# A decoder layer with 16384 experts on one core: the dense half of the tokens moved from the middle to the end

## The chip, the core and the metric

The kernel runs on one core of a Trainium2 chip. A core has a tensor engine (PE; its weight loads are shown apart as PEld), a vector engine (DVE), a scalar engine (ACT), GpSimd (POOL) and a queue engine for transfers (SP). Each works through its own instructions in a fixed order and waits on semaphores for the others. Sixteen DMA engines move data between DRAM and the core; SP starts the plain transfers here, POOL the gathers by index. The metric is the device time of one execution in microseconds; lower is better.

## The reference

One layer for 1024 tokens of width 1024, all in float32: a norm, a mixer of three branches (stick-breaking attention, sparse attention in three forms, a gated linear recurrence), a merge with sigmoid gates, an output projection, a second norm, a feed-forward part with product keys, a final norm. The change concerns the feed-forward part:

```python
qh = (xc @ w_q).reshape(Ct, H, 2, PEER_QDIM // 2)
s = jnp.einsum("nhad,akd->nhak", qh, sub_keys).astype(f32)
top_s, top_i = lax.top_k(s, K)
...
best_s, pos = lax.top_k(cand, K)
eidx = jnp.take_along_axis(cand_idx, pos, axis=-1)
gate = jax.nn.softmax(best_s, axis=-1)
ug = u_tab[eidx]
vg = v_tab[eidx]
hpre = jnp.einsum("nd,nhkd->nhk", xc, ug).astype(f32)
act = (gate * jax.nn.gelu(hpre, approximate=False)).astype(x.dtype)
return jnp.einsum("nhk,nhkd->nd", act, vg)
```

Each token has 8 heads of 16 experts, that is 128 of the 16384 experts; each expert has a row of 1024 numbers in `u_tab` and one in `v_tab`.

## The kernel before

The tokens go through the mixer in four parts of 256 (`PARTS`, parts 0 to 3), one after the other. Work is emitted in steps: a step takes the next stage of several branch chains (*items*), and fills up with *pieces* that stand on their own (projections, norms, merges, scores, routes) up to an estimate of vector and tensor work (`account`, L1054). A part's *tail* (`tail_pieces`: merge of the branches, output projection, second norm; then `score_pieces` and `routes`) is placed beside the next part's items by `place_tail` (L1262). The tail of the last part has no such place; its pieces go into a list, `ending`.

A scheduler with a simulated timeline then fixes each engine's order of instructions; on the chip this order doesn't change.

The experts are computed in two ways, each for half of the tokens.

*Gathered* (`gather_tile`, L1095, a tile of 128 tokens at a time). For each of the 128 places in the list, POOL gathers a row of `u` for every token (L1104: 128 rows of 1024 numbers, called a row here), and the vector engine multiplies it with the token's activations and sums (L1106). After a Gelu and the gates, 128 rows of `v` follow (L1114), each multiplied and added to the sum (L1116). Tiles of four parts would be eight; four are gathered: 4 x 256 = 1024 rows. The rows share five buffers (tag `rows`, `RB`), one of which holds the token tile's input or its running sum. `paced` (L1075) ties a row's arithmetic to a step of the mixer, so that it isn't issued before: 420 rows from step 135 on, in proportion to a step's tensor work; the others are free after the last step.

*Dense* (L1326 on). The tokens of `DENSE = PARTS[1:3]` (L65) go through all experts, in 128 blocks of 128 experts: a first product (`gemm1`, L1327: U block times the tokens' activations in two float16 parts, 24 matmuls of 512 columns, then Gelu), a multiplication with the gates spread over all experts (L1368), a split in two float16 parts (L200 and L201, tile `ac`), a second product with the V block (`gemm2`, L1375, 24 matmuls), accumulated in seven eighths over all blocks in PSUM, the rest added by the vector engine (L1383). First products run three blocks ahead (`LEAD`). The spread gates come from `spread_pieces` (L1158): for every four tokens four one-hot operations on the vector engine (L1168 to L1171, tile `hot`), eight matmuls (L1174, L1175), a copy (L1177), and for every sixteen tokens a store of 1 MB to `d_G`.

Since the last part isn't dense, the dense blocks can start when part 2 has its routes and its spread gates. The last part's tail is put between the blocks, three pieces of `ending` to a block (`TP`, L1388), and its two tiles are gathered after that.

Of the kernel before, what the change touches and what calls it, by code (L numbers as in the profile page):

```python
# [10 lines left out]
F32 = mybir.dt.float32  # L11
# [25 lines left out]
# operands of the large products are split into two float16 parts after scaling by these powers of two  # L37
# [4 lines left out]
# scales of the gates, of their spread over the experts, and of the activations in the dense experts  # L42
# [5 lines left out]
# block numbers in the stream of projection weights  # L48
# [5 lines left out]
class Part:  # L54
    """a run of tokens that goes through the mixer together"""
# [8 lines left out]
# the parts whose tokens go through all experts; the others' experts are gathered  # L64
DENSE = PARTS[1:3]  # L65
# [4 lines left out]
def trunk(ctx: ExitStack, tc: tile.TileContext, a: dict, out: bass.AP):  # L70
# [13 lines left out]
    # what the mixer alone needs  # L84
# [44 lines left out]
    # strictly causal block in reversed key order: key 127 - x, allowed where 127 - x < p  # L129
# [3 lines left out]
    # causal block: key x allowed where p - x >= 0  # L133
# [3 lines left out]
    # for each length of segments: keys of a first half before queries of the second, the second halves' queries only  # L137
# [7 lines left out]
    # distances to the keys of the window and to the ends of the blocks, negative; far under where the key isn't seen  # L145
# [11 lines left out]
    # lower bounds: cumulative softmax over the layers less the first layer's share  # L157
# [12 lines left out]
    # the window's keys and values: this part's and the one's before  # L170
# [27 lines left out]
    def split(hi, lo, src, scale):  # L198
        """src * scale in two float16 parts"""
# [3 lines left out]
    def rms_scale(src, name, junk, tg=""):  # L203
        """1/sqrt(mean(src^2) + eps) for each of 128 rows of 1024."""
# [15 lines left out]
    def load_w(blk, name, pt, br=False):  # L220
        """a block of weights in two parts; split for the first part, kept in DRAM for the others"""
# [29 lines left out]
    def transposed(src, name, pre=False):  # L251
        """the 128-column blocks of src transposed, side by side in one bank"""
# [11 lines left out]
    def norm_rows(xt, gname, nm):  # L264
        """RMSNorm of one token tile"""
# [5 lines left out]
    def norm_cols(ht, hh, hl, tl, kk, scale, nm):  # L271
        """half of a token tile transposed into columns of hh / hl"""
# [8 lines left out]
    own_h2 = {}  # L281

    def h2_cols(pt):
        if pt.last:
            if not own_h2:
                own_h2[0] = htp.tile([128, 2, 8, pt.n], F16, tag="hT", name="h2_last")
            return own_h2[0][:, 0], own_h2[0][:, 1]
        c = (pt.t0 - TD) % TH
        return h2[:, 0, :, c:c + pt.n], h2[:, 1, :, c:c + pt.n]
# [7 lines left out]
    # Work comes in two kinds. Pieces stand on their own (projections, norms, merges); items are steps of the  # L297
    # branches' chains, each cut into four stages so that several can be under way at once.
# [37 lines left out]
    def sb_pieces(p, pt, st):  # L336
# [3 lines left out]
        def keep(t, d):  # L340
            # the tokens of earlier parts come back from DRAM
# [10 lines left out]
        # keys and values in reversed token order  # L352
# [19 lines left out]
    def sb_items(p, pt, st):  # L372
# [3 lines left out]
        def chunk(tl, hh, c0, c1, W):  # L376
# [62 lines left out]
    def nsa_kv_pieces(pt, st):  # L439
# [22 lines left out]
        # compression of keys and values: block c takes the pieces c and c + 1 of 16 tokens.  # L462
        # Two neighbouring positions lie one under the other on the partitions; columns: position pair, group, block
# [3 lines left out]
        def pieces(which):  # L467
# [13 lines left out]
            # the last piece is kept for the next part  # L481
# [48 lines left out]
    def nsa_items(g, tl, pt, st, kv):  # L530
# [9 lines left out]
        # compressed branch  # L540
        def c_logits():
# [6 lines left out]
            # a column of nothing before the first block  # L548
# [19 lines left out]
        def c_select():  # L568
            # importance of the blocks: the heads' weights of the five pieces that overlap; sure blocks at the top
# [926 lines left out]
```

## Time and profile before

| | us |
|---|---|
| median of the runs | 3744.84 |
| lowest, highest | 3733.98, 3757.71 |
| span of the profiled execution | 3722.6 |
| PE busy | 3285.9 |
| DVE busy | 3035.8 |
| ACT busy | 1572.2 |
| POOL busy | 1275.4 |

The profile shows one execution: for each instruction its line, its engine, the program's names of what it writes and reads (`out<-in`), its start and duration, and what ended the idle time before it. Times in a trace are counted from the span's start. The executions hold the span and some time around it. "Busy" of the tensor engine includes the latency of pipelined matmuls. The granted clock is the share of its full clock that the tensor engine ran at.

### The profile page before, as it was taken

The page shows a single profiled execution, that of the slowest core. Times are in us where ns is not written, and L with a number is a line of the kernel's source. Part 1 is how long each engine was busy: PE and PEld are TensorE (multiplying, and loading weights), DVE is VectorE, ACT ScalarE, POOL GpSimd, SP SyncE. Part 2 cuts the span into 40 slices and gives each one's busy share as a digit, 9 for nine tenths or more (in the row PEclk, how much of TensorE's full clock was granted, in tenths as well). Part 3 has the DMA queues.
Part 4 walks back from the last instruction along what each step waited for, and adds up shares of the span by engine and source line. Part 5 has one row for each costly group of instructions (what it writes and reads, how often), then busy time and mean ns, then how long its engine had stood idle before and what let it go on. Part 6 is the DMA issues. An engine that isn't in the chain of part 4 may idle for free. (4 is left out here: it accounts for less than half of the span.)

```text
span 3722.6 us, 57637 instructions
## 1 busy us (share of the span) xinstructions
PE 3285.9 (88%) x20660; PEld 2191.0 (59%) x20660; DVE 3035.8 (82%) x7067; ACT 1572.2 (42%) x3110; POOL 1275.4 (34%) x1167
## 2 busy tenths in 40 slices
PE   6999999999986999898878897859999999999993
PEld 5887777777875777786566453424444444444441
DVE  5665689788799888789988678988888887888886
ACT  4776456554444564554457223323232223223222
POOL 0000002343322432233222344144555554555554
PEclk9999999999995999898577999979999999999996
DMA  7964857889974878877465999579999999999987
GB/s 260 334 243 144 295 189 274 317 308 325 328 273 147 300 256 300 296 278 261 142 208 195 356 332 325 193 273 339 333 337 325 320 337 322 346 332 318 334 287 261
DMA packets 359916, 1055.48 MB, mean 284 GB/s; under 512 B 35814, under 2 KB 108330, under 8 KB 355532
## 3 DMA queue, kind: packets, MB, share of 16 engines
q0 software_dynamic: 147456, 536.94, 41.5%
q1 hardware_dynamic: 212172, 514.86, 38.7%
q8 instruction: 162, 2.65, 0.3%
q14 instruction: 126, 1.03, 0.1%
HBM read 943.66 MB, written 108.00 MB: 283 GB/s over the span
## 5 line engine op out<-in xcount | busy, mean ns | idle before, releaser
L1114 POOL DMA_INDIRECT v<-in_peer_v_dram,gidx x512 | 655.1, 1280 | 872.7 <-DVE gacc L1116 590.8
L1104 POOL DMA_INDIRECT u<-in_peer_u_dram,gidx x512 | 605.9, 1183 | 869.1 <-DVE u L1106 599.4
L242 PE MATMUL g<-h,us 128*128 128x512 f16 x3072 | 712.5, 390 | 109.0 <-DVE acc L1383 71.4
L1116 DVE SCALAR_TENSOR_TENSOR gacc<-v,act,gacc 128x1024 f32<-128x1024 f32 x512 | 654.6, 1278 | 112.2 <-DMA v<-in_peer_v_dram,gidx 104.8
L1106 DVE SCALAR_TENSOR_TENSOR u<-u,gh 128x1024 f32<-128x1024 f32 x512 | 618.1, 1219 | 124.6 <-DMA u<-in_peer_u_dram,gidx 123.2
L242 PEld LDWEIGHTS <-us 128*128 128x128 f16 x3072 | 306.1, 100 | 497.8 <-issue 115.4
L1375 PE MATMUL acc<-vs,ac 128*128 128x512 f16 x2304 | 536.3, 384 | 33.1 <-ACT ac L200 28.4
L1375 PEld LDWEIGHTS <-ac 128*128 128x128 f16 x3072 | 302.9, 99 | 414.2 <-ACT ac L200 30.9
L242 PE MATMUL pj_mg<-hT,w_mg 128*128 128x256 f16 x2304 | 279.1, 277 | 16.3 <-ACT mg L859 9.5
L242 PEld LDWEIGHTS <-w_mg 128*128 128x128 f16 x2304 | 229.5, 101 | 48.8 <-issue 20.7
L200 ACT ACTIVATE vs<-vraw 128x1024 f16<-128x1024 f32 x128 | 133.8, 1048 | 270.3 <-DMA vraw<-in_peer_v_dram 270.1
L200 ACT ACTIVATE ac<-ge 128x512 f16<-128x512 f32 x128 | 79.9, 626 | 365.8 <-DVE ge L1368 250.0
L1335 ACT ACTIVATE ge<-g 128x512 f32<-128x512 f32 x128 | 75.6, 590 | 362.7 <-PE g L242 362.6
L1375 PE MATMUL g<-vs,ac 128*128 128x512 f16 x768 | 179.5, 385 | 9.6 <-DVE ts L958 7.3
L201 DVE SCALAR_TENSOR_TENSOR vs<-vraw,vs 128x1024 f16<-128x1024 f32 x128 | 155.2, 1217 | 23.2 <-ACT vs L200 23.2
L1174 PE MATMUL gb<-hot 128*128 128x128 f16 x512 | 126.3, 295 | 44.6 <-ACT stage L1177 28.9
L1177 ACT ACTIVATE stage<-gb 128x512 f32<-128x512 f32 x128 | 131.9, 1070 | 79.0 <-DMA d_G<-stage 45.2
L200 ACT ACTIVATE us<-uraw 128x1024 f16<-128x1024 f32 x128 | 134.0, 1049 | 68.2 <-DMA uraw<-in_peer_uT_dram 52.6
L242 PE MATMUL pb<-o,w_b 128*128 128x256 f16 x1152 | 141.6, 279 | 19.4 <-DMA w_b<-dw 9.3
L201 DVE SCALAR_TENSOR_TENSOR us<-uraw,us 128x1024 f16<-128x1024 f32 x128 | 155.7, 1218 | 2.9 <-ACT us L200 2.7
L242 PE MATMUL pj_r_hg<-hT,w_r_hg 128*128 128x256 f16 x1152 | 138.2, 277 | 1.5 <-ACT iv_hg L715 0.7
L242 PEld LDWEIGHTS <-w_b 128*128 128x128 f16 x1152 | 113.8, 101 | 42.6 <-issue 14.5
(1133 smaller groups left out, 5944.0 us busy)
## 6 DMA issues: line engine op xcount, KB each, us to landing
uraw<-in_peer_uT_dram SPq DMA_DIRECT2D x128, 512.0 KB, 6.7
vraw<-in_peer_v_dram SPq DMA_DIRECT2D x128, 512.0 KB, 6.2
w_mg<-dw SPq DMA_DIRECT2D x72, 512.0 KB, 6.3
d_G<-stage SPq DMA_DIRECT2D x32, 1024.0 KB, 5.1
gt<-d_G SPq DMA_DIRECT2D x32, 1024.0 KB, 13.2
w_r_hg<-dw SPq DMA_DIRECT2D x36, 512.0 KB, 5.7
w_b<-dw SPq DMA_DIRECT2D x72, 256.0 KB, 5.9
wr_mg<-in_wblk_dram SPq DMA_DIRECT2D x24, 512.0 KB, 5.1
```

The costliest lines, as they stand in the source:

```text
L200: S.activation(hi, src, AF.Copy, scale=scale)
L201: V.scalar_tensor_tensor(lo, in0=src, scalar=scale, in1=hi, op0=ALU.mult, op1=ALU.subtract)
L242: P.matmul(ps, l[:, k, :], r[:, k, :], start=(i == 0), stop=(i == n - 1))
L1104: G.indirect_dma_start(out=ur, out_offset=None, in_=a["peer_u"], in_offset=bass.IndirectOffsetOnAxis(ap=idx[:, c:c + 1], axis=0))
L1106: V.scalar_tensor_tensor(ur, in0=ur, scalar=1.0, in1=h2, op0=ALU.mult, op1=ALU.mult, accum_out=hpre[:, c:c + 1])
L1114: G.indirect_dma_start(out=vr, out_offset=None, in_=a["peer_v"], in_offset=bass.IndirectOffsetOnAxis(ap=idx[:, c:c + 1], axis=0))
L1116: V.scalar_tensor_tensor(acc, in0=vr, scalar=act[:, c:c + 1], in1=acc, op0=ALU.mult, op1=ALU.add)
L1174: P.matmul(ps[:, n, :], hs[:, 0, :, n], hs[:, 2, :, n], start=True, stop=False)
L1177: S.activation(stage[0][:, :, m0:m0 + 4].rearrange("p i n -> p n i"), ps, AF.Copy, scale=SA / SGT)
L1335: S.activation(ge, ps, AF.Gelu, scale=1.0 / (SW * SH2))
L1375: P.matmul(ps, ac[:, x, t * 128:(t + 1) * 128], v[:, y, dh * 512:(dh + 1) * 512], start=start and n == 0, stop=stop and n == 2)
```

## The change

`DENSE` becomes parts 2 and 3; parts 0 and 1 are gathered. The last part then needs routes and spread gates before the first dense block can use them, and its activations before a first product can be made. What follows the mixer's items is therefore arranged anew:

- The last part's merge, output projection and second norm are emitted alone, piece by piece.
- Then 28 first products (`NRUN`) are made; their results are kept in DRAM (`d_ge`). Beside each, pieces of the last part's scores, routes and spread are emitted until the vector engine's estimated work since the start reaches 7 us (`RUNV`) a block; what is left follows the 28th.
- The dense loop loads these 28 results instead of computing them (`made`), and computes the others as before. No tail pieces are left in it.
- The gathered rows are paced anew. A row may be due in a step when its tile has its routes (`ready_`), and rows are laid out in proportion to a step's tensor work beyond its vector work, with the steps now counted through the dense blocks, so that all 1024 are due at 94% of the steps (`ROWS_BY`).
- `account` estimates both engines' work in another way, which steers where pieces are placed.
- The last part's spread products use other PSUM buffers (tag `z`), and its activations lie in the tile `h2` with part 2's.

Comments and docstrings are left out in the changed kernel. The core of the diff:

```diff
-PACE0, PACE, PB = 135, 420, 3.0
-TP, LEAD = 3, 3
+LEAD, NRUN, RUNV = 3, 28, 7.0
+ROWS_BY = 0.94
...
-DENSE = PARTS[1:3]
+DENSE = PARTS[2:4]
...
             if i.engine == mybir.EngineType.DVE:
-                load_["DVE"] += 0.06 + max([...] or [0]) / 960.0
+                aps = [x for x in [*i.outs, *i.ins] if len(getattr(x, "ap", ())) > 1]
+                n = max([math.prod([x[1] for x in o.ap[1:]]) for o in aps] or [0])
+                half = aps and all(o.dtype in (F16, BF16) for o in aps)
+                load_["DVE"] += 0.09 + n / (1920.0 if half else 960.0)
...
-            def rows(tau):
-                return [tau * (p + PB) if k >= PACE0 else 0.0 for k, (_, v, p) in enumerate(marks)]
+            spare = [max(p - v, 0.0) for _, v, p in marks[:int(len(marks) * ROWS_BY)]]
+            tiles = sorted(ready_.values())
+            known = [256 * sum(r < k for r in tiles) for k in range(len(spare))]
+            def fill(f):
+                acc, res = 0.0, []
+                for w, n in zip(spare, known):
+                    acc = min(acc + f * w, n)
+                    res.append(acc)
+                return res
...
-            paces.append(marks[-1][0])
+            paces.append(marks[len(spare)][0])
...
             nc.sync.dma_start(d_gate[ti], gate)
+            ready_[ti] = len(marks) + 2
             return
...
-            ps = ps_mm.tile([128, 4, 128], F32, tag="mm", name=f"gb{n0}")
+            ps = (ps_z if pt.last else ps_mm).tile([128, 4, 128], F32, tag="z" if pt.last else "mm", name=f"gb{n0}")
...
+    def tail_step():
+        ending.pop(0).emit(1 << 20)
+        mark()
+    for _ in range(len(state[PARTS[-1].i, "tail"][0]) + len(state[PARTS[-1].i, "tail"][1])):
+        tail_step()
...
+    d_ge = []
+    account()
+    base = load_["DVE"]
+    while ending or len(d_ge) < NRUN:
+        if len(d_ge) < NRUN:
+            i = len(d_ge)
+            d_ge.append(dram(f"d_ge{i}", (128, TH)))
+            nc.sync.dma_start(d_ge[i], gemm1(i))
+            mark()
+        while ending and (len(d_ge) == NRUN or load_["DVE"] < base + len(d_ge) * RUNV):
+            tail_step()
+    mixing[0] = False
+    def made(i):
+        if i >= NRUN:
+            return gemm1(i)
+        return load(W2(f"ge{i}"), d_ge[i])
...
         if k + LEAD < NI:
-            ges[order[k + LEAD]] = gemm1(order[k + LEAD])
+            ges[k + LEAD] = made(k + LEAD)
+            mark()
...
-        while ending and gone < (k + 1) * TP:
-            ending.pop(0).emit(1 << 20)
-            gone += 1
+        mark()
```

More of the change, by code (lines that the diff above doesn't have):

```diff
@@ L1282, in place_tail @@
         if pt in DENSE:
-            kept = chain([lambda tl=tl: keep_route(pt.ti0 + tl) for tl in range(pt.nt)], -10, dl(3), rt[-1:] + laid, True)
-            laid[:] = chain(spread_pieces(pt), -10, 1 << 30, kept[-1:], True)[-1:]
+            kept = chain([lambda tl=tl: keep_route(pt.ti0 + tl) for tl in range(pt.nt)], -10, dl(3), rt[-1:] + laid, True, to=to)
+            laid[:] = chain(spread_pieces(pt), -10, 1 << 30, kept[-1:], True, to=to)[-1:]
     for pt in PARTS:
@@ L1336, in gemm1 @@
         return ge
[L1338 removed]
+    d_ge = []
[14 more added lines that the diff above has]
+        return load(W2(f"ge{i}"), d_ge[i])
     ges = {}
     for k in range(LEAD):
[L1341 removed]
+        ges[k] = made(k)
     mix.close()
@@ L1351, in trunk @@
     gts = {}
-    gone = 0
-    for k, i in enumerate(order):
+    for k in range(NI):
+        i = k
         if k + LEAD < NI:
-            ges[order[k + LEAD]] = gemm1(order[k + LEAD])
+            ges[k + LEAD] = made(k + LEAD)
+            mark()
         raw = load(late.tile([128, D], F32, tag="vraw", name=f"vraw{i}", bufs=2), a["peer_v"][i * 128:(i + 1) * 128, :])
```

28 lines of the change are left out of this document (12 added, 16 removed).

## The prediction

> **What bounds the kernel now.** I read the page first, then the stretches between marks that both kernels share, then the waits.
>
> ```profile
> span 3722.6 us, 57637 instructions
> PE 3285.9 (88%) x20660; PEld 2191.0 (59%) x20660; DVE 3035.8 (82%) x7067; ACT 1572.2 (42%) x3110; POOL 1275.4 (34%) x1167
> DVE  5665689788799888789988678988888887888886
> q0 software_dynamic: 147456, 536.94, 41.5%
> ```
>
> No engine is full. The tensor engine's 88% counts pipelined matmuls as busy. The vector engine, at 82%, works in order and runs nearly evenly after the first fifth. The gathered rows (queue q0) alone take 41.5% of the DMA engines' span: 0.415 x 3722.6 / 1024 rows = 1.51 us a row.
>
> I cut the trace at vector operations that exist in both kernels: the start of head 2 of part 2 (1086.3 us), of head 3 of part 3 (1869.8), the split of block 32's activations (2582.77), that of block 127 (3661.42). Columns are busy us (and instructions) of each engine, granted clock, DMA share, GB/s.
>
> ```profile
> 540.90:1086.30 545.40, 512.45 (x4046) 423.06 (x4047) 472.58 (x1425) 281.66 (x691) 189.99 (x204) 0.97 0.84 299
> 1086.30:1869.80 783.50, 684.78 (x4798) 557.51 (x4795) 694.85 (x2072) 392.05 (x867) 242.19 (x234) 0.85 0.73 250
> 1869.80:2045.00 175.20, 142.74 (x923) 114.66 (x921) 148.67 (x379) 113.95 (x194) 36.35 (x32) 0.73 0.56 195
> 2045.00:2582.50 537.50, 443.65 (x2274) 229.23 (x2275) 447.70 (x989) 146.23 (x198) 208.31 (x173) 0.92 0.85 302
> 2352.10:2469.10 117.00, 95.20 (x430) 43.45 (x429) 107.56 (x410) 38.08 (x48) 25.66 (x23) 0.92 0.56 187
> 2582.50:3661.20 1078.70, 1006.89 (x4541) 449.51 (x4540) 896.00 (x1165) 298.26 (x387) 574.19 (x438) 0.97 0.92 325
> 3661.20:3722.60 61.40, 14.80 (x69) 6.49 (x67) 39.68 (x61) 20.50 (x30) 18.35 (x18) 0.65 0.73 252
> ```
> ```profile
> 2582.77 0.69 DVE L201 SCALAR_TENSOR_TENSOR ac<-ge,ac 128x512 f16<-128x512 f32 x1
> ...
> 3661.42 0.69 DVE L201 SCALAR_TENSOR_TENSOR ac<-ge,ac 128x512 f16<-128x512 f32 x1
> ```
>
> From 1086.3 to 2582.5 the vector engine is busy 694.85 + 148.67 + 447.70 = 1291 of 1496 us, 86.3%, while the tensor clock sinks to 0.73: the vector engine leads there. From 2582.5 on, 95 dense blocks take 11.35 us each; DMA at 92%, tensor and vector engine all come close to their limits.
>
> ```profile
> DVE u L1106 <- DMA u<-in_peer_u_dram,gidx: 123.2, 106, 4.8
> DVE gacc L1116 <- DMA v<-in_peer_v_dram,gidx: 104.8, 89, 3.7
> ```
> ```profile
> PE g L242 <- DVE acc L1383: 71.4, 20, 10.6
> ```
> ```profile
> POOL u L1104 <- DVE u L1106: 599.4, 297, 18.4
> POOL v L1114 <- DVE gacc L1116: 590.8, 289, 17.7
> ```
>
> So the in-order vector engine waits 228 us for rows, the tensor engine waits behind it, and the gather waits for the vector engine to give buffers back.
>
> **What the change moves.** Both kernels have the same number of vector and tensor instructions; only 56 transfers are new. What differs is the order, so I count the changed kernel's built order between the same marks. Up to 1086.3 us it holds 164 rows for 165 and otherwise the same work: no change. From block 32 to block 127 it holds 437 rows for 437 and the same matmuls: I carry over 1078.7 us. The difference lies in between and after.
>
> Row work on the vector engine, first u rows (L1106; each counts twice, with its accumulator read), then v rows (L1116):
>
> ```profile
> 1086.30:2582.50 1496.20, 223.44 (x367) 0.86 0.75 262
> ...
> ```
> ```profile
> 1086.30:2582.50 1496.20, 279.47 (x219) 0.86 0.75 262
> ...
> 3661.20:3722.60 61.40, 24.67 (x20) 0.65 0.73 252
> ```
>
> By the orders, that middle stretch holds 184 + 219 rows before and 132 + 220 after: 51 fewer. A u row is 223.44 / 183.5 = 1.22 us, a v row 279.47 / 219 = 1.28. All other vector work in the stretch is the same. Its busy time becomes 1291 - 52 x 1.22 + 1.28 = 1229 us. The 51 rows, and one from the early difference, reappear behind the last block: 71 rows follow block 127's split, 19 did.
>
> *The middle stretch, in four pieces.* Prices of single operations:
>
> ```profile
> L201 DVE SCALAR_TENSOR_TENSOR us<-uraw,us 128x1024 f16<-128x1024 f32 x128 | 155.7, 1218 | 2.9 <-ACT us L200 2.7
> L201 DVE SCALAR_TENSOR_TENSOR vs<-vraw,vs 128x1024 f16<-128x1024 f32 x128 | 155.2, 1217 | 23.2 <-ACT vs L200 23.2
> L1368 DVE TENSOR_TENSOR ge<-ge,gt 128x256 f32<-128x256 f32 x256 | 100.2, 429 | 41.2 <-DMA gt<-d_G 34.1 <-ACT ge L1335 7.0
> L201 DVE SCALAR_TENSOR_TENSOR ac<-ge,ac 128x512 f16<-128x512 f32 x128 | 87.3, 683 | 3.8 <-ACT ac L200 3.8
> ```
> ```profile
> 1086.30:1869.80 783.50, 77.14 (x560) 63.86 (x560) 109.72 (x296) 0.85 0.73 250
> ```
> ```profile
> 2252.00:2480.00 228.00, 44.57 (x274) 0.91 0.75 261
> ```
> ```profile
> 3655.12 13.11 PE L1375 MATMUL acc<-vs,ac 128*128 128x512 f16 x60
> ```
>
> The second fence is the one-hot tile (tensor, load, vector): 109.72 / 296 = 0.371 us an operation. The third is what the vector engine spends on the last part's scores and their sixteen best. The fourth gives 0.2185 us for a 512-column matmul.
>
> 1. *Last merge, output projection, second norm* (now ahead of every dense block). 23 u rows (28 us) and small operations (24) make 52 us of vector work. The tensor engine has 288 + 192 matmuls of 256 columns, 480 x 0.109 = 52 us. Each alone needs over 52, one after the other 104. Before, dense blocks lay beside this chain; now only rows do. I take 80.
> 2. *Scores, routes, spread, with 28 first products beside them.* Vector: 61 v rows 78, 28 u rows 34, 256 one-hot operations 95, 28 weight splits 34, scores 45, routes some 35 (an estimate: 107.56 us of the stretch at 2352.1, less rows, blocks and scores): 320 us. Tensor: 28 x 24 x 0.2185 = 147, and 512 gate products of 128 columns and the score products some 85 (an estimate, at half that rate), 232 in all, hidden under the vector engine. The 28 stores, 7.3 MB, lie in some 90 MB that this piece moves; 360 us at 325 GB/s would carry 117. A store stands in SP's queue ahead of the next weights' loads and holds them until its Gelu is done; that is hidden while the vector engine is behind, and could cost one landing a block if it were not. At the vector share of 1869.8 (148.67 / 175.2 = 84.9%, spread) 377 us, at that of 2352.1 (107.56 / 117 = 91.9%, routes) 348; I take 360.
> 3. *Blocks 0 to 31*, 28 of them without their first product: tensor 936 x 0.2185 = 205; vector 71 rows 90, splits 39 + 22, gate products 21, sums 6, 178 in all; DMA 71 rows 37 MB, v blocks 17, u blocks 4, gates 8, kept products 7: 73 MB at 325 GB/s, 225. I take 235.
> 4. *What is left*, the mixer of parts 2 and 3 without part 1's spread: 1229 - 52 - 320 - 178 = 679 us of vector work. At 86.6% (stretch from 540.9) to 88.7% (694.85 / 783.5) 784 to 766; with part 2's spread in it, nearer the first: 783.
>
> Together 80 + 360 + 235 + 783 = 1458, against 1496: **38 us saved**. It could be nothing (all at 82%), or 183 (below).
>
> *The tail.* 52 more rows after block 127, with no tensor work beside them. Bounds for one: 1.51 us, its DMA share; from above, the end of the present trace:
>
> ```profile
> 3668.18 5.25 DVE L1116 SCALAR_TENSOR_TENSOR gacc<-v,act,gacc 128x1024 f32<-128x1024 f32 x4 [1.17 <-DMA v<-in_peer_v_dram,gidx]
> ...
> 3677.44 1.28 DVE L1116 SCALAR_TENSOR_TENSOR gacc<-v,act,gacc 128x1024 f32<-128x1024 f32 x1 [0.50 <-DMA v<-in_peer_v_dram,gidx]
> ...
> 3695.89 1.28 DVE L1116 SCALAR_TENSOR_TENSOR gacc<-v,act,gacc 128x1024 f32<-128x1024 f32 x1
> ```
> ```profile
> u<-in_peer_u_dram,gidx POOLq DMA_INDIRECT x512, 6.4
> v<-in_peer_v_dram,gidx POOLq DMA_INDIRECT x512, 6.4
> ```
>
> From 3677.44 nine rows take 18.45 us, 2.05 each, the final norm of the dense tokens between them. Four that had landed go at 1.31, but five buffers, one of them the sum, cannot keep that up. I take 1.78, the middle: 52 x 1.78 = **93 us added** (79 to 107).
>
> [...]
>
> Sum: -38 + 93 = +55 on the profiled span of 3722.6. The median of the runs shown (3744.84) is 22 us above the span; I keep that.
>
> **The rivals.** *The vector engine fills up: faster.* The point of the order is that dense products lie beside work that only the vector engine does, and rows beside work of both. If the middle stretch ran at the vector share of the present one's best piece,
>
> ```profile
> 1086.30:1243.90 157.60, 120.28 (x725) 95.27 (x723) 147.87 (x467) 68.87 (x169) 49.38 (x49) 0.73 0.62 211
> ```
>
> 147.87 / 157.6 = 93.8%, it would take 1229 / 0.938 = 1310, saving 186: -186 + 93 = -93, 3652 us. It wins from a share of 1229 / (1496 - 93) = 87.6% on. For it: rows never run out any more, where the present kernel has few between routes at 2352 us (DMA 0.56). Against it: present pieces of that kind stand at 84.9 to 91.9%, the whole at 86.3%, and pieces 1 and 3 are not vector-bound.
>
> *The gain pays for the tail: no change.* At shares of 85.3 to 90% the net lies within 37 us of zero, the middle 3745.
>
> *The tensor clock.* The granted clock is 0.85 and 0.73 where the vector engine leads. If the tensor engine set piece 2, feeding it would be the gain: 360 would become its floor, the vector engine's 320, the net +15, 3760 us. But 148.67 of 175.2 us are vector work at 0.73 already. [...]
>
> *More than forecast*: the kept products' loads and the gate tiles block SP's queue in blocks 0 to 31, and the norm of piece 1 stands alone. At both upper ends (104 and, at the present 11.35 us a block, 363) these two add 24 + 128 = 152; half of it, the likelier, makes +55 + 76 = +131, 3876 us.
>
> **How the numbers follow.** Forecast with its spread, 3770 to 3835: 0.42; more than that 0.16; no change 0.15 and the clock's case, which ends there too, 0.05; faster 0.22. About 1%, 37 us, is what can be told from no change. Slower by over 1% is then 0.58, within 0.20, faster 0.22. The likeliest is 3745 + 55 = 3800. The range leaves out a tenth on each side: 3680 to 3870; the likeliest case's own is 3770 to 3835.
>
> **What would show it.** Right: at the split of block 32 some 38 us earlier than 2582.77; 51 fewer rows by then; 11.35 us a block after it; some 70 rows behind the last block with PE idle, at 1.5 to 2.05 us each. Wrong: a vector share over 90% between 1086 us and block 32; rows at 1.3 us in the tail; or dense blocks whose pace changes from 11.35 us, which I carried over.

## The result, and the profile after

The changed kernel takes 3895.17 us (median; 3890.46 to 3902.78) where the kernel before takes 3744.03 beside it: a ratio of 1.0402, 95% interval 1.037 to 1.0433. It is slower by 4%. The direction was forecast, the size was not: 3895 lies above the range's upper end of 3870.

The profiled execution has a span of 3897.5 us, 174.9 more than before. The medians differ by 151 us; the profiled execution of the kernel before was a short one of its kind, so the profiles differ by 24 us more. The page's head, tensor and vector engine by slices of 97 us, and the gathers' queue:

```profile
span 3897.5 us, 57900 instructions
...
PE 3304.1 (85%) x20660; PEld 2184.9 (56%) x20660; DVE 3050.1 (78%) x7067; ACT 1578.2 (40%) x3111; POOL 1306.3 (34%) x1167
...
PE   6999999999988899979777685898999998999940
...
DVE  5665698887796877996769985787888887878875
...
q0 software_dynamic: 147456, 536.94, 40.1%
```

The work is nearly the same: tensor and vector engine are busy for 18 and 14 us more, the bytes of the gathers are equal. Most of the 175 us is idle time of both engines. The slices say where: the vector engine is at 6 or 7 tenths from the 19th to the 21st, which are the end of the mixer and the last merge, and at 5 in the 25th, where the last part's spread ends; and in the last slice the tensor engine has stopped.

The changed kernel cut at the marks of the prediction, and at four more: the last merge (1953.0), the first split of a first product's weights (2033.1), the last part's first one-hot operation (2193.7), the split of block 0's activations (2430.9). Columns as in the prediction (PE, PEld, DVE, ACT, POOL busy, clock, DMA share, GB/s):

```profile
1093.00:1778.40 685.40, 607.17 (x4305) 483.08 (x4306) 569.02 (x1752) 346.99 (x810) 197.10 (x192) 0.88 0.68 233
1778.40:1953.00 174.60, 149.78 (x960) 120.88 (x959) 121.92 (x342) 109.38 (x192) 8.53 (x9) 0.74 0.35 127
1953.00:2033.10 80.10, 59.36 (x499) 50.28 (x498) 54.02 (x124) 11.01 (x27) 26.05 (x25) 0.90 0.95 340
2033.10:2193.70 160.60, 106.38 (x545) 57.74 (x543) 150.43 (x576) 38.61 (x53) 54.63 (x50) 0.81 0.75 251
2193.70:2430.90 237.20, 166.51 (x877) 98.02 (x878) 171.90 (x344) 95.03 (x106) 68.16 (x41) 0.75 0.75 253
2430.90:2653.00 222.10, 201.68 (x896) 89.13 (x895) 177.32 (x216) 65.67 (x82) 101.23 (x72) 0.95 0.92 320
2653.00:3734.70 1081.70, 1002.67 (x4501) 446.87 (x4500) 892.95 (x1216) 298.70 (x387) 561.57 (x438) 0.96 0.92 324
3734.70:3897.50 162.80, 16.52 (x77) 7.31 (x75) 106.13 (x113) 20.60 (x30) 85.89 (x71) 0.56 0.78 264
```

Against the prediction's terms (us):

| stretch | before | forecast | after |
|---|---|---|---|
| up to head 2 of part 2 | 1086.3 | 1086.3 | 1093.0 |
| piece 4: mixer from there to the last merge | | 783 | 860.0 |
| piece 1: last merge, projection, norm | | 80 | 80.1 |
| piece 2: scores, routes, spread, 28 first products | | 360 | 397.8 |
| piece 3: blocks 0 to 31 | | 235 | 222.1 |
| the four together | 1496.2 | 1458 | 1560.0 |
| block 32 to block 127 | 1078.7 | 1078.7 | 1081.7 |
| behind it | 61.4 | 154 | 162.8 |

So the middle gave +64 where -38 was forecast, a miss of 102 us, and nearly all of it lies in pieces 4 (+77) and 2 (+38). The vector engine is busy for 1244.6 of the 1560.0 us, 79.8%; the prediction had let this share fall no lower than to 82%. The tail came out at +101 for +93. Runs 1 and 10 below, with the same order of work in the middle, took 1557 us each for it, so this miss is no scatter between executions; a single piece does scatter (piece 4 took 852 and 862 us there).

Two places show what the pieces meet. In the last part's spread (2193.7 to 2430.9), the waits of scalar, vector and tensor engine (us in total, times, longest):

```profile
ACT stage L1189 <- DMA d_G<-stage: 48.3, 14, 7.9
...
ACT us L201 <- DMA uraw<-in_peer_uT_dram: 29.7, 14, 9.4
```
```profile
DVE hot L1180 <- PE gb L1187: 39.2, 22, 4.3
```
```profile
PE gb L1186 <- ACT stage L1189: 21.9, 17, 5.5
```

A ring is to be read here: the scalar engine may not copy gates into the one collecting tile (`stage`) until its store has landed; the tensor engine may not write its PSUM tile until the copy is done; the vector engine may not overwrite its one-hot tile until the tensor engine has read it. In these waits the vector engine isn't the slow one; it is the last link of a wait for one buffer. The 29.7 us for weights (`uraw`) are a wait of another kind, which run 10 returns to. In the tail, the operations on the running sum and two waits:

```profile
L1127 DVE SCALAR_TENSOR_TENSOR gacc<-v,act,gacc x70: 1274/1284/1343, 3740.7 to 3886.2; 128x1024 f32<-128x1024 f32 x70
```
```profile
DVE gacc L1127 <- DMA v<-in_peer_v_dram,gidx: 44.7, 40, 3.8
```
```profile
POOL v L1125 <- DVE gacc L1127: 33.6, 28, 3.4
```

Seventy rows start over 145.5 us, 2.11 each where the arithmetic takes 1.28: the vector engine waits for a row, the gather waits for the vector engine's buffer, and the dense tokens' final norm lies between the rows.

### The profile page after: what moved, and what is told of

The parts are those of the page before. It is cut to its first block, busy times and chain, and to the rows that moved or that the text cites. A ratio compares the mean times of both kernels' runs of the same rounds, so it can differ in the third digit from the quotient of the medians.

```text
span 3897.5 us, 57900 instructions
## 1 busy us (share of the span) xinstructions
PE 3304.1 (85%) x20660; PEld 2184.9 (56%) x20660; DVE 3050.1 (78%) x7067; ACT 1578.2 (40%) x3111; POOL 1306.3 (34%) x1167
## 4 chain that ended last, share of the span: by engine, by line
issue 24%; PE 23%; DMA 18%; DVE 18%; POOL 11%; ACT 6%; SPq 0%; POOLq 0%; DVEq 0%; ACTq 0%
DMA v<-in_peer_v_dram,gidx 11%; POOL u L1115 7%; POOL v L1125 4%; PE pj_mg L243 4%; DMA u<-in_peer_u_dram,gidx 3%; DVE gacc L1127 3%; PE pj_r_hg L243 2%; PE g L243 2%; DVE u L1117 2%; PE pb L243 2%; DMA d_G<-stage 1%; PE pj_wo L243 1%; DVE sv L951 1%; DVE ts L953 1%; DVE ts L957 1%
## 5 line engine op out<-in xcount | busy, mean ns | idle before, releaser
L1125 POOL DMA_INDIRECT v<-in_peer_v_dram,gidx x512 | 668.1, 1305 | 893.9 <-DVE gacc L1127 672.3
L1115 POOL DMA_INDIRECT u<-in_peer_u_dram,gidx x512 | 623.4, 1217 | 1005.8 <-DVE u L1117 784.9
L243 PE MATMUL g<-h,us 128*128 128x512 f16 x3072 | 741.2, 400 | 156.2 <-DVE acc L1423 81.7
```

Source lines behind the costliest of these rows:

```text
L243: P.matmul(ps, l[:, k, :], r[:, k, :], start=(i == 0), stop=(i == n - 1))
L1115: G.indirect_dma_start(out=ur, out_offset=None, in_=a["peer_u"], in_offset=bass.IndirectOffsetOnAxis(ap=idx[:, c:c + 1], axis=0))
L1125: G.indirect_dma_start(out=vr, out_offset=None, in_=a["peer_v"], in_offset=bass.IndirectOffsetOnAxis(ap=idx[:, c:c + 1], axis=0))
```

## The experiments

Each run's time is compared with the changed kernel's 3895.17 us. The ratio behind it, with its 95% interval, is to the kernel before as measured beside that run (medians of 3738 to 3747 us). Stretches are cut at the same vector operations; the first cut of runs 3 and 5 lies 1.3 us behind that operation.

**1. The last 52 rows left out.**

```diff
-        for c in range(128):
+        for c in range(76 if ti == 3 else 128):
```

> The changed kernel, but the last gathered tile leaves out its last 52 rows of v (that part of the sum is missing from the output of tile 3). It measures the tail. By the forecast's term a row behind the last block costs 1.78 us, so 93 us less: about 3802 us. If the rows there only cost their vector time of 1.28 us, 67 us less: 3828. If the end is set by something else (the dense tokens' final norm), under 30 us less.

3798.27 us (ratio to before 1.0134, 1.0077 to 1.0192): 97 us less for 52 rows, 1.86 each. The stretch behind block 127 is the one of before (61.4) again:

```profile
3729.20:3791.80 62.60, 14.80 (x69) 6.51 (x67) 39.40 (x61) 20.50 (x30) 20.52 (x19) 0.64 0.73 254
```

The tail's term stands: mechanism and price are as forecast. What is left, 1.3% over the kernel before, is the middle.

**2. A second collecting tile for the last part's spread** (in a buffer that is free by then).

```diff
-                stage[0] = per.tile([128, 128, 16], F32, tag="stage", ...)
+                if pt.last and q // 4 % 2:
+                    stage[0] = htp.tile([128, 128, 16], F32, tag="hT", ...)
+                else:
+                    stage[0] = per.tile([128, 128, 16], F32, tag="stage", ...)
```

> The changed kernel, but every second store of the last part's spread gates comes out of a tile of another ring (two buffers, tag hT), so that the copy of the next sixteen tokens needn't wait for the store before. Theory A, the single stage buffer bounds the spread from 2194 to 2431 us (237 us for 172 us of vector work): the piece shrinks towards 172 / 0.9 = 190, about 40 us less, 3855. Rival, the chain of one-hot operations, products and copies bounds it anyhow, or what is saved there is lost in the dense blocks: less than 10 us, 3885 to 3905.

3843.59 us (1.0276, 1.0213 to 1.034): 52 us less. The last part's spread and blocks 0 to 31:

```profile
2175.10:2388.30 213.20, 155.96 (x877) 96.57 (x878) 171.79 (x345) 98.15 (x107) 70.93 (x41) 0.81 0.82 284
2388.30:2592.50 204.20, 189.38 (x847) 84.35 (x846) 173.70 (x212) 63.19 (x79) 99.98 (x69) 0.95 0.93 331
```
```profile
ACT stage L1192 <- DMA d_G<-stage: 1.4, 1, 1.4
```

The same vector work (171.8 us) now takes 213 instead of 237 us, and the wait for the store has gone from 48.3 to 1.4. The blocks behind gain 18, though they took 215 us in runs 9 and 10 too, without the tile, so 7 of the 18 may be scatter. That makes 35 to 42 us for the tile; this profile is also 19 us earlier where the spread starts, before anything was changed, so that much is scatter between executions. Piece 2 comes to 158.9 + 213.2 = 372 us, 12 from the forecast.

**3. All rows due at 85% of the steps.**

```diff
-ROWS_BY = 0.94
+ROWS_BY = 0.85
```

> The changed kernel with all rows due at 85% of the steps instead of 94%: in the built order 57 more rows lie up to the end of the mixer's items, 82 more up to block 32, and none behind block 127 (71 before). Theory B, the middle isn't bound by the vector engine any more (its share there fell to 80%), so that rows find room in its waits: the tail's 101 us go, the middle grows by at most 40: 3795 to 3855. Rival, forecast's own view that vector work sets the middle: 82 rows cost 1.25 us each there, 102 us, and the time stays at 3880 to 3910.

3849.62 us (1.0283, 1.0226 to 1.0339): 46 us less. The tail is down to 44 us, but 51 more of the rows now lie in the mixer from head 2 of part 2 to head 3 of part 3:

```profile
1090.00:1815.80 725.80, 609.54 (x4251) 484.51 (x4249) 622.76 (x1849) 344.70 (x807) 253.61 (x242) 0.85 0.75 255
```

There they cost 725.8 - 685.4 = 40 us, 0.79 each. The whole middle, up to block 32, holds 76 rows more and takes 72 us more (1632.5 for 1560.1 us), 0.95 each, where the expectation had allowed 40 us. A row is dear behind the last block (1.9) and cheaper, not free, ahead of it.

**4. No early products.**

```diff
-LEAD, NRUN, RUNV = 3, 28, 7.0
+LEAD, NRUN, RUNV = 3, 0, 7.0
```

> The changed kernel with no first products ahead (0 instead of 28): the last part's scores, routes and spread go by themselves, all 128 first products are made in the dense loop. Theory: 28 blocks go from some 6 to 11.35 us, up to 140 us more; routes and spread lose 28 weight splits (34 us) and rows, 398 us become 290 to 340; 19 more rows in the tail, 27 to 38 us: 60 to 120 us slower, 3955 to 4015. Rival, the early products only move vector and DMA work from one place to another: within 20 us of 3895 plus the tail's share, 3900 to 3950.

3901.4 us (1.0407, 1.0353 to 1.0461), within 6 us of the changed kernel. From the last merge to block 0, then blocks 0 to 31:

```profile
1942.40:2284.00 341.60, 183.05 (x1353) 146.65 (x1350) 257.32 (x925) 94.68 (x125) 48.64 (x43) 0.70 0.52 191
2284.00:2609.30 325.30, 311.43 (x1421) 139.90 (x1422) 276.52 (x308) 99.99 (x130) 176.30 (x127) 0.98 0.94 331
```

The first is 136 us shorter (477.9 in the changed kernel), the second 103 longer; the dense blocks and the tail take the rest back. The first also holds 73 gathers fewer (43 for 25 + 50 + 41), which come later, so products and rows aren't parted here. Taken together they cost beside the spread about what they save later: the early products are no cause of the loss, and no gain.

**5. No rows tied to the mixer from head 2 of part 2 on.**

```diff
+            for k in range(start[2, 2, "hg"], N + 3):
+                spare[k] = 0.0
```

> The changed kernel, with no gathered row tied to any step of the mixer from head 2 of part 2 on. From that mark to head 3 of part 3 its order holds 27 rows where the changed kernel's holds 161 (134 fewer), all of them free rows; the rows come later, 178 of them behind the last block's split (71 before). Nothing is left out. What this tells: what the mixer stretch (685 us in the changed kernel, 569 us of it vector work) would be if the vector engine had still less to do. Theory A (the vector engine's share is constant, as in the prediction): 134 rows x 1.25 us = 168 us less vector work, at the present 83% some 200 us less: about 485 us. Theory B (in that stretch the work that was taken out lay partly beside a wait that stays): by the step from the kernel before, 98 us for 126 us of vector work, 0.78 each: 168 x 0.78 = 130, about 555 us. Theory C (a floor of another chain is reached, the tensor and scalar engines' stages one after the other): 620 to 660 us, that is 25 to 65 us less. The tail should take some 160 + 107 x 1.9 = 360 us by all of them, so that the whole is slower than the changed kernel by up to 150 us, or even with it by theory A.

4088.0 us (1.0935, 1.0891 to 1.098), with 357 us of tail. The stretch in question:

```profile
1090.20:1729.60 639.40, 574.60 (x4285) 467.10 (x4284) 416.97 (x1534) 335.91 (x798) 36.45 (x57) 0.91 0.40 137
```
```profile
DVE e_sb L392 <- ACT e_sb L387: 75.0, 23, 10.4
```

152 us less vector work saved 46 us; the other 106 are idle time of the vector engine. The largest part of it, some 45 us, is its wait for the scalar engine within the attention (`e_sb`), which in the changed kernel was

```profile
DVE e_sb L392 <- ACT e_sb L387: 29.5, 10, 9.2
```

Four runs of one stretch, head 2 of part 2 to head 3 of part 3, now give a rough price for vector work (us):

| run | DVE busy | length | saved per us of DVE against the line above |
|---|---|---|---|
| before | 694.85 | 783.5 | |
| rows by 85%, no spread of part 1 | 622.76 | 725.8 | 57.7 / 72.1 = 0.80 |
| the changed kernel | 569.02 | 685.4 | 40.4 / 53.7 = 0.75 |
| no rows | 416.97 | 639.4 | 46.0 / 152.1 = 0.30 |

The prediction had divided by a share of 86.6 to 88.7%, which is 1.13 to 1.15 us saved for each. The prices are rough in two ways. In the first step part 1's spread left as well, with 547 matmuls and 47 us of the scalar engine's work. And a length is that of one execution: runs 1, 2, 4 and 10, with the changed kernel's order in this stretch, took 683, 678, 674 and 687 us. With these the second price lies between 0.75 and 1.0, so that it can't be told from the first, and the third between 0.2 and 0.3.

**6. Gates in float16, two collecting tiles for both spreads; 7. the same with rows by 85%; 8. the same gates in the kernel before.**

```diff
-    d_G = dram("d_G", (32, 128, 128, 16))
+    d_G = dram("d_G", (32, 128, 128, 16), F16)
...
-                stage[0] = per.tile([128, 128, 16], F32, tag="stage", ...)
+                stage[0] = per.tile([128, 128, 16], F16, tag="stage", ..., bufs=2)
```

(and the tile `gt` in float16.)

> The changed kernel, with the spread gates kept in float16 in place of float32 (the tile that collects sixteen tokens, its store of now 0.5 MB, and the loads of the gates beside the dense blocks), and with two such tiles instead of one, for both parts' spreads. The gates lose the bits that float16 doesn't hold. Theory A (the single collecting tile and its store bound both spreads): the stretch from head 3 of part 3 to the last merge falls from 174.5 to 140..150 us, the last part's spread from 237 to 195..213 us, blocks 0 to 31 from 222 to 200..210 us, and the dense blocks gain a little by the halved gate loads (8 MB less in all): 60 to 90 us less than the changed kernel's, about 3805 to 3835. Theory B (the spread is bound by the vector engine's one-hot operations and the tensor engine's waits for them): under 20 us gained, above 3875.

> The kernel with half-size gates and two collecting tiles, and with all rows due at 85% of the steps instead of 94%, so that none is left behind the last block. If the two gains add up (45 us from the rows, as measured alone; 60 to 90 from the gates): about 3760 to 3790. If the rows that move into the middle use the very time that the collecting tile's waits left free, they add up to less: 3800 or more. Either way the changed order stays at or above the kernel before unless the first holds at its lower end.

> The kernel before, with the spread gates in float16 and two collecting tiles, as in the run of the changed kernel with half-size gates. There the last spread (part 2's) lies beside part 3's mixer, from head 3 on and before block 0. Theory A (the collecting tile bounds the stretch from head 3 to the last merge, 175.2 us, in the kernel before too): 20 to 50 us gained, about 3700 to 3725, which would be below both kernels. Theory B (there the vector engine bounds it, with 148.67 of 175.2 us busy): 0 to 15 us gained.

3875.38 us (1.0377, 1.0331 to 1.0424), 3845.78 (1.0285, 1.0232 to 1.0337) and 3765.79 (1.0074, 1.0044 to 1.0103). The gains hoped for are missed in all three: 20 us for 60 to 90, 4 us beside run 3, and the kernel before 0.7% slower. The groups of instructions, for part 2's spread (1772.2 to 1965.1 with float16, 1778.4 to 1953 in the changed kernel):

```profile
L1189 ACT ACTIVATE stage<-gb 128x512 f16<-128x512 f32 x56 | 131.1, 2447 | 8.3 <-PE gb L1187 8.2
```
```profile
L1189 ACT ACTIVATE stage<-gb 128x512 f32<-128x512 f32 x56 | 56.3, 1067 | 31.6 <-DMA d_G<-stage 18.5 <-PE gb L1187 13.1
```

The wait for the store is gone, and the copy itself takes 2447 ns instead of 1067: it writes single elements with fifteen others between them, and in float16 this is slower by more than the wait was long. The stretch grew from 174.6 to 192.9 us. The runs confound two things and say nothing on what a second float32 tile would do for part 2's spread; none was tried there.

**9. The old work estimate steers the mixer's pieces; 10. the stores of products and gates started by the scalar engine.**

```diff
+                load2_["DVE"] += 0.09 + n / (1920.0 if half else 960.0)
+                load_["DVE"] += 0.06 + n / 960.0
...
+                load_["PE"] += n / 2400.0 * (4 if i.ins[0].dtype == F32 else 1)
```
```diff
-            nc.sync.dma_start(d_ge[i], gemm1(i))
+            nc.scalar.dma_start(d_ge[i], gemm1(i))
...
-                nc.sync.dma_start(d_G[n0 // 16], stage[0])
+                (nc.scalar if pt.last else nc.sync).dma_start(d_G[n0 // 16], stage[0])
```

(In run 9 `load2_`, the new estimate, serves the pacing and the pieces beside the products.)

> The changed kernel with one part undone: the placing of the mixer's pieces is steered by the old estimate of both engines' work, while the pacing of the rows and the pieces beside the first products go on by the new one. The rows stand within 6 of the changed kernel's at every mark. Theory A (the new estimate misplaces the mixer's pieces and so lengthens the stretch from head 2 of part 2 to head 3 of part 3, 685 us): 30 to 60 us gained there, the whole at 3835 to 3865. Theory B (the stretch is at the mixer's own floor, by the run without rows 639 us, plus the rows' part): within 15 us of the changed kernel.

> The changed kernel with the 28 stores of first products and the 16 stores of the last part's spread gates started by the scalar engine instead of the queue engine SP, so that no store stands ahead of a weight load in SP's queue. Theory A (SP's queue is held up, the prediction's rival named more than forecast: uraw loads end 29.7 us of the scalar engine's waits between the last part's spread and block 0): the stretch from the last part's spread to block 0, 237 us, falls by 15 to 30 us. Theory B (the collecting tile's store is what is waited for, whoever starts it): within 8 us there. In blocks 0 to 31 nothing changes by either.

3898.29 us (1.0443, 1.0394 to 1.0492) and 3899.68 (1.0407, 1.0362 to 1.0453). Nothing moved: the mixer stretch takes 683.1 us with the old estimate, the last part's spread 240.5 with the stores moved, and its wait for the tile stays (scalar engine's waits, 2190 to 2440):

```profile
ACT stage L1189 <- DMA d_G<-stage: 48.4, 14, 7.7
...
ACT us L201 <- DMA uraw<-in_peer_uT_dram: 37.2, 12, 13.0
```

Neither the new estimate nor SP's queue is a cause; the wait for weights (`uraw`) that ended 29.7 us of the scalar engine's idle time is not shortened by it either.

**11. Runs 2 and 3 together; 12. and the stores from the scalar engine.**

> The two repairs that gained alone, together: a second collecting tile for the last part's spread (52 us alone) and all rows due at 85% of the steps (45 us alone). If they add up: 3895 - 97 = 3798, 3785 to 3810; the spread's stretch 215..225 us, the tail 40. If the rows fill just the time that the second tile frees: 3820 to 3845. Above the kernel before by either.

> The same with the stores started by the scalar engine too. If SP's queue is a cost of its own: another 10 to 30 us less than the two repairs together, some 3770 to 3790, still above the kernel before. If not: within 8 us of it.

3827.58 us (1.0223, 1.0191 to 1.0254) and 3821.65 (1.0219, 1.0179 to 1.026). Of 97 us, 68 are gained: the rows that leave the tail take up part of what the second tile had freed. The stores again add nothing that can be told. Run 12 is the fastest form of the changed order among these runs, and the kernel before stays ahead of it by 2%.

**13 to 15. About 500 tensor products less in the mixer,** in the changed kernel, in that without rows (run 5) and in the kernel before: of the three float16 products of each merge gate projection of parts 2 and 3 only the first is made.

```diff
-            for l, r in ((wh, ah), (wh, al), (wl, ah)):
+            for l, r in ((wh, ah),) if one else ((wh, ah), (wh, al), (wl, ah)):
...
+        if one:
+            load_["PE"] += 16 * 0.11
```

(Calls for parts 2 and 3 set `one`; the added estimate, 16 * 256 / 2400.0 in the kernel before, keeps the pieces where they were. The scheduler moves 9, 9 and 13 rows across the first mark.)

> The changed kernel with one of three float16 products left out of... rather: with only the first of the three float16 products of the merge gates' projections for parts 2 and 3 (16 of 24 matmuls of 256 columns in each are left out, some 500 in the stretch from head 2 of part 2 to head 3 of part 3, about 55 us of tensor time at 0.109 each); the pieces are placed as if they were there. All vector work stays. Theory A (two engines near their limits: tensor 607 and vector 569 of 685 us busy, each paid for at about 0.6 us per us): 25 to 40 us less up to head 3 of part 3. Theory B (the vector engine alone bounds it, as the prediction had it): within 8 us of the changed kernel's 1778. Theory C (the tensor engine alone): 50 us or more less.

> The same products left out of the kernel with no rows in the mixer, where the stretch took 639.3 us with the tensor engine busy for 575 and the vector engine for 417. Theory A or C (the tensor engine's work is the floor): 40 to 55 us less, 585 to 600. Theory B (a chain of single steps between the engines is the floor): under 20 us less.

> The same products left out of the kernel before (head 3 of part 3 at 1869.8 us; vector engine busy 694.9 of 783.5 us, tensor engine 684.8). By the prediction's reading (the vector engine leads there): within 10 us of 1870. If both engines share the bound there too: 25 to 40 us less; the products of the stretch after it, up to the last merge, gain a few us more.

3889.27, 4068.49 and 3712.5 us, of one execution each, 6, 20 and 31 us less than with all the products. The stretch from head 2 of part 2 to head 3 of part 3 in the three:

```profile
1080.90:1773.10 692.20, 579.06 (x3765) 452.87 (x3763) 579.40 (x1760) 355.10 (x815) 197.48 (x202) 0.82 0.68 236
```
```profile
1074.80:1717.20 642.40, 549.61 (x3735) 433.04 (x3733) 426.50 (x1546) 346.22 (x801) 43.81 (x67) 0.84 0.41 141
```
```profile
1068.80:1856.20 787.40, 646.01 (x4313) 512.08 (x4312) 709.32 (x2085) 392.95 (x868) 262.71 (x248) 0.83 0.74 259
```

540, 550 and 485 matmuls fewer, 53 to 60 us at 0.109 (in the kernel before 24 such matmuls in a row, `pj_mg` from 1247.72 us on, take 2.62 us up to the next one's start), and the stretch doesn't get shorter: 692, 642 and 787 us for 685, 639 and 784. The rows that moved into it (10, 10 and 14 us more vector work) are worth some 8, 3 and 12 us at the prices above, so the products gave between nothing and 8 us, within the scatter. Tensor work alone doesn't set this stretch either, though the tensor engine is busy for 90% of it without rows. The test is weaker than the count of products says: with the granted clock lower (0.82 for 0.88, 0.84 for 0.91, 0.83 for 0.85), the engine's busy time fell by 28, 25 and 39 us only.

Outside that stretch the products do count. From head 3 of part 3 to the last merge run 13 takes 162 us with the same vector work and 86 matmuls fewer, where the six profiles of the changed order with all the products (the changed kernel's and those of runs 1, 2, 4, 9 and 10) took 168 to 175. The stretch ahead of head 2 of part 2 (from the prediction's cut at 540.9 us on), from which the rows had moved, got shorter as well: 542 us for 551 to 562, 538 for 552 and 526 for 545. There products and rows aren't parted.

What remains to suspect is the order itself: single steps that alternate between engines, each engine with other work in its fixed order between them. Five lines of the timeline of run 5 (start, duration, engine, what waited for what) show one branch:

```profile
1402.30 0.56 DVE L639 CUSTOM_DVE_ANT_0 e_ns3g0t0b1h<-z_ns3g0t0b1h,zero 128x384 f32<-128x384 f32 x1 [0.90 <-PE ob_ns3g0t0b1h L665]
...
1402.90 0.16 DVE L642 TENSOR_TENSOR nmx_ns3g0t0b1h<-nmx_ns3g0t0b1h 128x1 f32<-128x1 f32 x1
1403.09 0.72 ACT L646 ACTIVATE e_ns3g0t0b1h<-e_ns3g0t0b1h,nmx_ns3g0t0b1h 128x512 f32<-128x512 f32 x1 [2.71 <-DVE nmx_ns3g0t0b1h L642]
...
1405.34 0.94 PE L654 MATMUL tre_ns3g0t0b1h<-ident,e_ns3g0t0b1h 128*128 128x128 f32 x7
...
1406.04 0.98 ACT L656 ACTIVATE eT_ns3g0t0b1h<-tre_ns3g0t0b1h 128x512 f32<-128x512 f32 x2 [1.10 <-PE tre_ns3g0t0b1h L654]
```

The vector engine waits for the tensor engine, the scalar engine for the vector engine, and then for the tensor engine again, which did other products (`pb`, `ob`) before this branch's `tre`. Followed back from the end through this stretch of run 5, the chain of waits and work lies on the tensor engine for 407 of 641 us, on the vector engine for 142 and on the scalar engine for 57, and changes engine some 50 times; in run 14 it is 351, 151 and 87 of 642. So the tensor engine has the largest part in the chain, and with fewer products other steps took the place of what was left out. That such chains hold the stretch at 640 us is argued from this and from the two removals; no run shortened a chain as a whole.

**16. Half tiles in the kernel before.** The collecting tile as two of eight tokens, stored one by one.

```diff
-            if q % 4 == 0:
-                stage[0] = per.tile([128, 128, 16], F32, tag="stage", ...)
+            if q % 2 == 0:
+                stage[0] = per.tile([128, 128, 8], F32, tag="stage", ..., bufs=2)
...
-                nc.sync.dma_start(d_G[n0 // 16], stage[0])
+                nc.sync.dma_start(d_G[n0 // 16][:, :, n0 % 16 - 4:n0 % 16 + 4], stage[0])
```

> The kernel before, with the tile that collects spread gates split in two of eight tokens each (together as large as the one), stored separately, so that one is filled while the other is stored; the stores write runs of 32 bytes instead of 64, and nothing is left out. If the single tile's wait is what the stretch from head 3 of part 3 to the last merge loses (30.0 us of the scalar engine's waits): 15 to 30 us gained, about 3715 to 3730, below the kernel before. If stores in short runs take longer than filling a tile: slower by 10 to 60 us.

4143.3 us (1.1079, 1.1038 to 1.112). The expectation's 64 bytes were wrong: a partition's share of the whole tile is one run of 128 x 16 x 4 = 8192 bytes, and it became 128 runs of 32. A store's way from issue to landing, of this run and then of the kernel before:

```profile
d_G<-stage SPq DMA_DIRECT2D x64, 512.0 KB, 20.8
```
```profile
d_G<-stage SPq DMA_DIRECT2D x32, 1024.0 KB, 5.1
```

Half the bytes take four times as long, and both spreads stand behind them: the scalar engine waits 340.6 us for these stores (45.2 in the kernel before), and the two mixer stretches that hold the spreads, up to head 3 of part 3 and from there to the first weight split (tile `us`), take 177 and 228 us longer. Both answers of the expectation, a gain and a loss of 10 to 60 us, were wrong.

## Why the prediction was wrong

- *Early stretch, no change.* Right but for 7 us: 1093.0 for 1086.3. Runs 1, 2 and 10, which have the same order up to there, end it at 1089.8, 1088.3 and 1088.6, so most of the 7 is scatter.
- *Piece 1, 80 us.* Right: 80.1. The 80 was taken between 52 and 104; that it fits so closely is luck.
- *Piece 3, 235 us.* 222, and 204 when the spread ahead of it was freed: 13 us too high.
- *Piece 4, 783 us, is the step that failed:* "679 us of vector work. At 86.6% ... to 88.7%". The vector work was nearly as counted (569.0 + 121.9 = 691), the share was not: 80%. A share is what a piece shows with a certain amount of work in it. It isn't a constant by which the piece shrinks when work is taken out. Taking out 126 us of vector work between head 2 of part 2 and head 3 of part 3 saved 98 us, not 145, and taking out more saved 0.2 to 0.3 us per us: the stretch came to a floor of about 640 us, which 25 us less busy time of the tensor engine didn't lower either. That chains of steps across the engines are this floor is argued, not shown. With the measured work at 86.6%, the two stretches of piece 4 would have taken 657 and 141 us; so of the 77 us that were missed 28 lie before head 3 of part 3, 34 behind it, and 15 come from vector work that was counted too low. From head 3 on, 175.2 us before and 174.6 after hold about the same (923 and 960 matmuls, 58 and 56 copies of gates); 27 us less vector work saved nothing there, or 7 us by the shortest of the six profiles. What sets this stretch stays open: run 13 shortened it with fewer products, run 6 lengthened it with slower copies. The scalar engine waited there for the store of the one collecting tile, before and after, which no run tested by itself:

```profile
ACT stage L1177 <- DMA d_G<-stage: 30.0, 9, 6.2
```
```profile
ACT stage L1189 <- DMA d_G<-stage: 18.5, 8, 4.9
```

- *Piece 2, 360 us, failed the same way:* its vector work was counted as 320 (150.4 + 171.9 = 322 measured) and divided by a share of 85 to 92%; it ran at 81%. The wait for the collecting tile had no term in the sum. Run 2 showed it in the share's place: with a second tile, 372, so 26 of the 38 us. Before, the spread had the mixer's work beside it; here little lay beside it but products, and the pace was that of the one buffer.
- *Dense blocks, 1078.7 carried over.* Right: 1081.7.
- *The tail, +93 (79 to 107).* Right: +101 in the profile, 97 by run 1. The mechanism is the forecast one, and a row's price is 1.86 us by run 1, in the upper half of the bounds; the 2.11 us from start to start in the profile, the final norm included, lie just above the upper one (2.05).
- *The rivals.* "The vector engine fills up" was refuted: its share fell to 79.8%, where 87.6% was needed. "More than forecast" came nearest with 3876, but by luck, from the wrong places: piece 1 and blocks 0 to 31 took no more than forecast, and moving the stores out of SP's queue gave nothing. The tensor clock went along with the waiting: in run 13 it sank from 0.88 to 0.82 and the stretch took 692 us for 685, with some 8 us of rows more. That it costs nothing in piece 2, where it was 0.81 and 0.75, is not shown.

In the sum, of the 120 us between forecast (+55) and profile (+175) 102 are the middle (77 + 38 by the two shares, less 13 in piece 3), 8 the tail, 10 the two stretches that were carried over. Against the medians the miss is 96 us (+151 for +55). The 22 us between span and median that the prediction kept were no fixed part of an execution: in the runs a time is some 2 us above its span, so the stretches before were those of a short execution. None of the prediction's signs of being wrong appeared (a vector share over 90%, rows at 1.3 us, another pace of the blocks: 79.8%, 1.86 and 1081.7 / 95 = 11.39 us); what told was the first sign of being right, which failed: block 32's split came 70 us later than 2582.77, not 38 earlier.

## What to carry to other kernels

When work is taken out of a piece in which two engines stand above 85% (here 87% and 89%), don't divide what is left by the old busy share: look for the next chain or single buffer beneath it, and price the saving from two pieces that differ in that work alone (here 0.75 to 1.0 us per us at first, 0.2 to 0.3 later, against 1.13 to 1.15 assumed). When a producer is moved to a place of its own, count how many buffers it hands over through; the wait for one store can become its pace when little other work lies beside it (here 48.3 us of such waits in a spread of 237 us, and 1.4 in 213 with a second tile). Independent transfers pushed behind the last block can cost more than their arithmetic, here 1.9 us a row for 1.28 of vector work, against 0.8 to 0.95 ahead of it.

## What the runs showed of the hardware

- A scalar engine copy of 128x512 from PSUM, whose elements go to every sixteenth place, took 1067 ns into float32 (the changed kernel) and 2447 ns into float16 (run 6).
- A store of 0.5 MB in runs of 32 bytes took 20.8 us from issue to landing (run 16), one of 1 MB in runs of 8 KB 5.1 us in the kernel before and 4.8 in the changed one.
- With 540 of 4305 matmuls taken out of a stretch of nearly the same length (692 for 685 us), the granted clock was 0.82 for 0.88, and the tensor engine's busy time fell by 28 us, where the matmuls count for 59 at 0.109 each (run 13). With 550 of 4285 taken out of the stretch without rows (642 for 639 us) the clock was 0.84 for 0.91, and the busy time fell by 25 us (run 14).
